# MLP entry of a hybrid decoder trunk: operand sums reordered, three kinds of sums moved to GpSimd, one buffer moved, lo*hi products last

## The chip, the cores and the metric

The kernel runs on one core of a Trainium2 chip. The metric is device microseconds of one launch, weights and input already in HBM. Three runs of the kernel before gave 2114.93, 2116.28 and 2116.18 us (median 2116.18).

## What is computed

Two decoder layers on 512 tokens of width 1024, all float32. Each layer: RMS norm, three parallel mixers, merge, output projection `w_out`, residual; then RMS norm and a gated MLP with a causal convolution:

```
x = x + merged @ w_out[l]
x = x + conv_ffn(rms_norm(x, ffn_norm_g[l]), w_up[l], conv_w[l], conv_b[l], w_down[l])

def conv_ffn(h, w_up, conv_w, conv_b, w_down):
    a, b = split(h @ w_up, 2, axis=-1)          # w_up is 1024 x 5632
    a = conv_b + sum(conv_w[j] * a shifted by 2 - j tokens for j in 0, 1, 2)
    return (silu(a) * b) @ w_down
```

The change touches the place where the second norm ends and `h @ w_up` begins, once per layer.

## The kernel before

Every float32 matrix product is made of three matmuls on split operands, x = hi + lo and w = hi + lo: hi·hi, hi·lo and lo·hi. ScalarE rounds to hi (`wsplit` line 163, `xsplit` line 506), VectorE subtracts to get lo (lines 164 and 507).

**The products of `w_up`.** For `h @ w_up` the kernel uses a seven-product scheme for 2x2 blocks in place of eight. x11 and x12 are tokens 0 to 255, with features 0 to 511 and 512 to 1023; x21 and x22 are tokens 256 to 511 with the same features. `fnorm_tile` (called for t = 0, 1, 2, 3, 128 tokens each) normalizes, transposes through TensorE into a `tp` bank of PSUM (two banks), and for t = 2 and 3 forms the sums s3 = x11 - x21, s1 = x22 - x21, s2 = -s1 - x11, s4 = -s2 - x12. All sums and all lo parts are VectorE's; the four operands "22", s1, s2, s3 lie in `hth`/`htl`, the others in tiles of their own (x11h, x12l, xs4h, xs4l). `ffn_quad` runs eleven times per layer (f = 0, 2, .. 20), each time over 256 columns of `w_up`: it loads four blocks of weights (w11, w12, w22, w21), forms four sums of them with `wsum` (VectorE, line 1111, into `tw` and in place), and calls `xprod` seven times with the operands "11", "s3", "s2", "12", "s1", "22", "s4". One `xprod` is 24 matmuls of 128x256 columns: for each half s and each k the three products in turn. x0 is the one PSUM bank with tag `o`; y0 and y1 are the two banks tagged `s`. `x0` of the next quad waits until `ua` (line 1139) has been copied out of it.

**Fillers.** For f = 0 `keep` issues twice eight bfloat16 matmuls that nobody reads (line 203), behind product "12" and behind the last transposes.

**Buffers.** `tw` is one of the six buffers tagged `raw`, in which the weight loads land too. The tag `gn` has one buffer: the norm's gain row.

**Order.** A framework takes the instructions in the order of the code and puts them, at build time, into one queue per engine, where it may move some ahead of others; each engine then works its queue strictly in order and waits on semaphores. `issue_after(i)` holds what is issued inside it behind instruction i. `later(2, rest)` puts the transposes and sums of a tile two steps later in the code.

Of the kernel before, what the change touches and what calls it, by code (L numbers as in the profile page):

```python
# [16 lines left out]
F32 = mybir.dt.float32  # L17
# [3 lines left out]
AF = mybir.ActivationFunctionType  # L21
ALU = mybir.AluOpType
AX = mybir.AxisListType.X
MUL, ADD, SUB, MAX, MIN = ALU.mult, ALU.add, ALU.subtract, ALU.max, ALU.min
# [24 lines left out]
class Stream:  # L49
# [3 lines left out]
    def __init__(self, gens, rate, depth=1):  # L53
        self.gens, self.rate, self.depth = gens, rate, depth
        self.credit, self.running = 0.0, []
# [29 lines left out]
class Net:  # L85
    def __init__(self, ctx, tc, io, out, depth, dbg=None):
        self.tc, self.nc, self.io, self.out, self.depth = tc, tc.nc, io, out, depth
        self.dbg = dbg or {}
        self.sb = ctx.enter_context(tc.tile_pool(name="sb", bufs=1))
        self.ps = ctx.enter_context(tc.tile_pool(name="ps", bufs=1, space=bass.MemoryType.PSUM))  # L90
        self.dr = ctx.enter_context(tc.tile_pool(name="dr", bufs=1, space=bass.MemoryType.DRAM))
        self.V, self.A, self.G, self.PE = tc.nc.vector, tc.nc.scalar, tc.nc.gpsimd, tc.nc.tensor
        self.specs = []
        self.after = []
        self.side, self.soon = [], []
        self.dq = tc.nc.sync
        self.n = 0

# [349 lines left out]
    def norm_rows(self, xt, t):  # L448

        V, A, G = self.V, self.A, self.G  # L450
        ss = self.small("nss", 2)
        for h in range(2):
            junk = self.slot("tmp", "junk")
            A.activation(junk, xt[t][h], AF.Square, accum_out=ss[:, h : h + 1])
        r = self.small("nr", 1)
        G.tensor_tensor(r, ss[:, 0:1], ss[:, 1:2], op=ADD)
        G.tensor_scalar(r, r, 1.0 / D, EPS, op0=MUL, op1=ADD)
        G.tensor_tensor(r, r, self.mhalf[:, 0:1], op=ALU.pow)
        hs = [self.slot("tmp", "hn") for _ in range(2)]
        for h in range(2):  # L460
            last = V.scalar_tensor_tensor(hs[h], xt[t][h], r, self.gn[:, h * 512 : h * 512 + 512], op0=MUL, op1=MUL)
        if self.after:
            self.after.append(last)
        return hs
# [32 lines left out]
        self.xop = ops  # L497
        self.x1 = self.slot("y4", "x11", (128, 4, 256)), self.slot("ct", "x12", (128, 4, 256))

    def xsplit(self, n, src, c):  # L500

        hi, lo = self.xop[n]
        w = 4 // len(hi)
        for i, (h, l) in enumerate(zip(hi, lo)):
            s = src[:, i * w : i * w + w]
            self.A.copy(h[:, :, c], s)
            self.V.tensor_tensor(l[:, :, c], s, h[:, :, c].bitcast(F32), op=SUB)

    def fnorm_tile(self, xt, t, wait=0):
        V, A = self.V, self.A  # L510
        hs = self.norm_rows(xt, t)
        x11, x12 = self.x1
        v4 = lambda a: a.rearrange("p (k q) -> p k q", k=4)

        def rest():
            c = slice((t % 2) * 128, (t % 2) * 128 + 128)
            tp = [v4(self.transpose4(hs[h])) for h in range(2)]
            if t < 2:
                for n, x, dst in zip(("11", "12"), tp, self.x1):
                    self.xsplit(n, x, c)  # L520
                    A.copy(dst[:, :, c], x)
                return
            x21, s3, s1, s2, s4 = (v4(self.slot("tmp", "xs")) for _ in range(5))
            A.copy(x21, tp[0])
            V.tensor_tensor(s3, x11[:, :, c], x21, op=SUB)
            self.xsplit("s3", s3, c)
            V.tensor_tensor(s1, tp[1], x21, op=SUB)
            V.scalar_tensor_tensor(s2, s1, -1.0, x11[:, :, c], op0=MUL, op1=SUB)
            self.xsplit("s2", s2, c)
            self.xsplit("s1", s1, c)  # L530
            self.xsplit("22", tp[1], c)
            V.scalar_tensor_tensor(s4, s2, -1.0, x12[:, :, c], op0=MUL, op1=SUB)
            self.xsplit("s4", s4, c)

        if wait:
            self.later(wait, rest)
        else:
            rest()
# [555 lines left out]
    def xprod(self, bank, w, n, start):  # L1094

        wh, wl = (x.rearrange("p (k f) -> p k f", k=4) for x in w)
        hi, lo = self.xop[n]
        per = 4 // len(hi)
        mm = self.PE.matmul
        for s in range(2):  # L1100
            o = bank[:, s * 256 : s * 256 + 256]
            fs = slice(s * 128, s * 128 + 128)
            for k in range(4):
                xh, xl = hi[k // per][:, k % per], lo[k // per][:, k % per]
                mm(o, lhsT=wh[:, k, fs], rhs=xh, start=start and s == k == 0, stop=False, skip_group_check=True)  # L1105
                mm(o, lhsT=wh[:, k, fs], rhs=xl, start=False, stop=False, skip_group_check=True)  # L1106
                last = mm(o, lhsT=wl[:, k, fs], rhs=xh, start=False, stop=k == 3, skip_group_check=True)  # L1107
        return last

    def wsum(self, out, a, b):  # L1110
        self.V.tensor_tensor(out, a, b, op=ADD)
        return out

    def ffn_quad(self, l, f, y0, y1, lo_out):


        V, A = self.V, self.A
        ca, cb = f * 128, DFF + f * 128
        w11 = self.load("s", "w_up", l, 0, ca)
        w12 = self.load("s", "w_up", l, 0, cb)  # L1120
        w22 = self.load("s", "w_up", l, 512, cb)
        tw = self.slot("raw", "tw", (128, 1024))
        w21 = self.load("s", "w_up", l, 512, ca)
        x0 = self.psum("o")
        self.xprod(x0, self.wsplit(w11), "11", True)
        A.copy(y0, x0)
        x1 = self.psum("tp")
        self.xprod(x1, self.wsplit(self.wsum(tw, w12, w22)), "s3", True)
        s7 = self.slot("tmp", "s7")
        A.copy(s7, x1)  # L1130
        self.xprod(y0, self.wsplit(self.wsum(tw, tw, w11)), "s2", False)
        A.copy(y1, y0)  # L1132
        last = self.xprod(x0, self.wsplit(w21), "12", False)
        if f == 0:
            self.keep(8, last)
            self.keep(8, self.last_tp)
        a = self.slot("ct", "ua", (128, 2, 512))
        half = lambda v: v.rearrange("p (s q) -> p s q", s=2)
        A.copy(a[:, :, :256], half(x0))
        self.xprod(y1, self.wsplit(self.wsum(w12, w12, w11)), "s1", False)  # L1140
        b2 = self.slot("tmp", "ub2")
        V.tensor_tensor(b2, y1, s7, op=ADD)
        self.xprod(y0, self.wsplit(self.wsum(tw, tw, w21)), "22", False)
        V.tensor_tensor(a[:, :, 256:], half(y0), half(s7), op=ADD)
        self.tick()
        self.xprod(y1, self.wsplit(w22), "s4", False)
        b1 = self.slot("tmp", "ub1")
        A.copy(b1, y1)
        y = self.slot("y4", "uy", (128, 2, 512))
        for s in range(2):  # L1150
            cw = lambda j: self.pk[:, l, PK_CW + 3 * (f + s) + j : PK_CW + 3 * (f + s) + j + 1]
            A.activation(y[:, s], a[:, s], AF.Identity, scale=cw(2), bias=self.pk[:, l, PK_CB + f + s : PK_CB + f + s + 1])
            V.scalar_tensor_tensor(y[:, s, 1:], a[:, s, :511], cw(1), y[:, s, 1:], op0=MUL, op1=ADD)
            V.scalar_tensor_tensor(y[:, s, 2:], a[:, s, :510], cw(0), y[:, s, 2:], op0=MUL, op1=ADD)
        A.activation(a, y, AF.Tanh, scale=0.5)
        V.scalar_tensor_tensor(y, a, 1.0, y, op0=ADD, op1=MUL)
        for h, b in enumerate((b1, b2)):
            yh = y[:, :, h * 256 : h * 256 + 256]
            V.tensor_tensor(yh, yh, half(b), op=MUL)
        gated = []  # L1160
        for s in range(2):
            hi, lo = self.slot("acc", "gh", dt=F32R), lo_out[:, s]
            A.activation(hi, y[:, s], AF.Copy, scale=-0.5)
            V.scalar_tensor_tensor(lo, y[:, s], -0.5, hi.bitcast(F32), op0=MUL, op1=SUB)
            gated.append((hi, lo))
        self.tick()
        return gated
# [242 lines left out]
```

## Time and profile before

| what | value |
|---|---|
| median of three runs | 2116.18 us |
| the profiled execution | 2114.53 us |
| its span, first to last instruction | 2112.8 us |
| TensorE (PE) busy | 2082.7 us, 99% |
| VectorE (DVE) busy | 1399.0 us, 66% |
| ScalarE (ACT) busy | 1002.1 us, 47% |
| GpSimd (POOL) busy | 156.4 us, 7% |

The profiled execution is 1.73 us longer than its span and 1.65 us below the median. A row of the timeline gives start, duration, engine, line, operation, out<-in, shape, and in brackets how long the engine had been idle before it and what released it. Durations overlap: an engine starts its next instruction before the last one's end, so that a 128x512 VectorE operation of 0.69 us costs 0.6 us of its queue and a 128x256 matmul of 0.28 us costs 0.12. The line "Lnnn" is of the kernel before; in the changed kernel the same code stands 1 to 12 lines further down.

### The profile page before, as it was taken

Reading aid. Unit: us, or ns where it says so; the run is one execution under the profiler, and the core shown is the slowest. Engines: PE = TensorE matmul, PEld = TensorE weight load, DVE = VectorE, ACT = ScalarE, POOL = GpSimd, SP = SyncE. Lnnn points to the kernel's source line nnn. Section 1 sums busy time; section 2 is a strip of 40 time slices with the busy share of each in tenths; the row PEclk is TensorE's granted clock in tenths of the full one; section 3 lists DMA queues with packets and bytes.
Section 4 is the critical chain, followed back from the end, with each engine's and each line's share of the span. In section 5 each row is a group of like instructions: output and inputs, shape, how many; then the busy total and the mean of one; then the engine's idle time right before and its main releaser. Section 6 shows DMA issues by size and latency. Waiting matters only on the chain.

```text
span 2112.8 us, 31791 instructions
## 1 busy us (share of the span) xinstructions
PE 2082.7 (99%) x12203; PEld 1821.6 (86%) x12203; DVE 1399.0 (66%) x2856; ACT 1002.1 (47%) x1981; POOL 156.4 (7%) x324
## 2 busy tenths in 40 slices
PE   9999999999999999999999999999999999999999
PEld 6877899988888799999878778999888888999997
DVE  7767565555645798888646675655565448987884
ACT  5355555553332555455443555454532326645552
POOL 1210112100000000000002111120000000000000
PEclk9999999999999999999999999999999999999999
DMA  6331222433332123323432311314334221333321
GB/s 211 99 94 39 70 78 63 121 123 102 138 100 74 66 95 120 110 92 108 154 111 72 101 41 61 96 46 143 110 100 146 94 70 56 105 110 111 110 91 70
DMA packets 97132, 206.09 MB, mean 98 GB/s; under 512 B 40530, under 2 KB 45394, under 8 KB 96980
## 3 DMA queue, kind: packets, MB, share of 16 engines
q1 hardware_dynamic: 96980, 204.06, 29.8%
q8 instruction: 96, 1.57, 0.3%
q14 instruction: 56, 0.46, 0.1%
HBM read 192.49 MB, written 11.53 MB: 97 GB/s over the span
## 4 chain that ended last, share of the span: by engine, by line
PE 87%; DVE 6%; ACT 4%; POOL 2%; issue 1%; DMA 1%; POOLq 0%; ACTq 0%; DVEq 0%
PE pacc L189 19%; PE pacc L188 19%; PE pacc L190 19%; PE ps L1105 4%; PE ps L1107 4%; PE ps L1106 4%; PE ptp L195 3%; PE po L1105 2%; PE po L1107 2%; PE po L1106 2%; PE ps L653 1%; PE po L750 1%; PE ptp L1106 1%; PE ptp L1105 1%; PE ptp L1107 1%
## 5 line engine op out<-in xcount | busy, mean ns | idle before, releaser
L164 DVE TENSOR_TENSOR wlo<-raw,whi 128x1024 fp32r<-128x1024 f32 x328 | 397.9, 1222 | 257.5 <-ACT whi L163 246.3
L163 ACT CAST whi<-raw 128x1024 fp32r<-128x1024 f32 x328 | 342.6, 1051 | 391.5 <-PE pacc L189 192.0
L188 PE MATMUL pacc<-whi,hth 128*128 128x512 f32 x768 | 319.1, 416 | 0.0
L189 PE MATMUL pacc<-wlo,hth 128*128 128x512 f32 x768 | 310.2, 404 | 3.2 <-DVE wlo L164 3.2
L190 PE MATMUL pacc<-whi,htl 128*128 128x512 f32 x768 | 310.9, 405 | 0.2 <-DVE htl L478 0.2
L189 PEld LDWEIGHTS pacc<-wlo,hth 128*128 128x128 f32 x768 | 192.6, 251 | 18.6 <-DVE wlo L164 4.1
L190 PEld LDWEIGHTS pacc<-whi,htl 128*128 128x128 f32 x768 | 191.7, 250 | 17.4 <-DVE htl L478 0.9
L188 PEld LDWEIGHTS pacc<-whi,hth 128*128 128x128 f32 x768 | 191.9, 250 | 15.7 <-ACT hth L477 0.4
L188 PE MATMUL pacc<-hth,whi 128*128 128x512 f32 x448 | 177.0, 395 | 0.0
L189 PE MATMUL pacc<-htl,whi 128*128 128x512 f32 x448 | 176.7, 394 | 0.0
L190 PE MATMUL pacc<-hth,wlo 128*128 128x512 f32 x448 | 174.6, 390 | 0.0
L1105 PE MATMUL ps<-hth,whi 128*128 128x256 f32 x528 | 148.3, 281 | 2.8 <-ACT ps L1132 2.8
L1107 PE MATMUL ps<-hth,wlo 128*128 128x256 f32 x528 | 147.6, 280 | 0.0
L1106 PE MATMUL ps<-htl,whi 128*128 128x256 f32 x528 | 147.6, 280 | 0.0
L189 PE MATMUL pacc<-wlo,gh 128*128 128x512 f32 x352 | 139.1, 395 | 0.0
L188 PE MATMUL pacc<-whi,gh 128*128 128x512 f32 x352 | 139.0, 395 | 0.0
L1105 PEld LDWEIGHTS ps<-hth,whi 128*128 128x128 f32 x528 | 99.2, 188 | 3.2 <-ACT ps L1132 3.2
L163 ACT CAST whi<-tw 128x1024 fp32r<-128x1024 f32 x66 | 69.3, 1049 | 67.3 <-PE po L1106 23.2
L188 PEld LDWEIGHTS pacc<-hth,whi 128*128 128x128 f32 x448 | 84.2, 188 | 19.1
L190 PEld LDWEIGHTS pacc<-hth,wlo 128*128 128x128 f32 x448 | 84.2, 188 | 18.5
L1107 PEld LDWEIGHTS ps<-hth,wlo 128*128 128x128 f32 x528 | 99.5, 188 | 0.0
L1106 PEld LDWEIGHTS ps<-htl,whi 128*128 128x128 f32 x528 | 98.9, 187 | 0.0
(373 smaller groups left out, 4675.0 us busy)
## 6 DMA issues: line engine op xcount, KB each, us to landing
raw<-wpk SPq DMA_DIRECT2D x328, 512.0 KB, 3.5
x<-x SPq DMA_DIRECT2D x16, 256.0 KB, 5.8
u_d<-uS SPq DMA_DIRECT2D x8, 256.0 KB, 2.4
u<-u_d SPq DMA_DIRECT2D x8, 256.0 KB, 3.4
y_d<-ys SPq DMA_DIRECT2D x8, 256.0 KB, 2.1
ym<-y_d SPq DMA_DIRECT2D x8, 256.0 KB, 4.0
um<-u_d SPq DMA_DIRECT2D x8, 256.0 KB, 3.4
oc_d<-glu SPq DMA_DIRECT2D x8, 256.0 KB, 2.0
```

Of the source, the lines that this page charges most:

```text
L163: self.A.copy(hi, raw)
L164: self.V.tensor_tensor(lo, raw, hi.bitcast(F32), op=SUB)
L188: self.PE.matmul(out, lhsT=ah, rhs=bh, start=i == 0, stop=False)
L189: self.PE.matmul(out, lhsT=ah, rhs=bl, start=False, stop=False)
L190: self.PE.matmul(out, lhsT=al, rhs=bh, start=False, stop=i == n - 1)
L195: self.last_tp = self.PE.transpose(tp[:, b * 128 : b * 128 + 128], src[:, b * 128 : b * 128 + 128], self.ident)
L653: PE.matmul(reg, lhsT=q[64 * j : 64 * j + 64, h * 128 : h * 128 + 128], rhs=k[kt][64 * j : 64 * j + 64, h * 128 : h * 128 + 128], start=kt ...
L750: PE.matmul(o[:, h * 128 : h * 128 + 128], lhsT=v[kb][:, h * 128 : h * 128 + 128], rhs=pT[:, c : c + 128], start=b == 0, stop=b == nb - 1)
L1105: mm(o, lhsT=wh[:, k, fs], rhs=xh, start=start and s == k == 0, stop=False, skip_group_check=True)
L1106: mm(o, lhsT=wh[:, k, fs], rhs=xl, start=False, stop=False, skip_group_check=True)
L1107: last = mm(o, lhsT=wl[:, k, fs], rhs=xh, start=False, stop=k == 3, skip_group_check=True)
```

## The change

It does five things. (1) `fnorm_tile` forms s3 of t = 2 and t = 3 first and puts all other sums of both into a list that is worked off after t = 3's; x22 is now copied from PSUM by ScalarE first. (2) x12 is kept negated, so that s4 = (-x12) - s2 is one plain subtraction, and s4 and its lo part are GpSimd's. (3) For f = 0 two of the four weight sums (w12 + w11 for product "s1", tw + w21 for product "22") are GpSimd's, held behind the last norm's reciprocal square root. (4) For f > 0 `tw` lies in the buffer `gn`. (5) `xprod` runs all eight hi·hi matmuls, then the eight hi·lo, then the eight lo·hi.

```diff
     def norm_rows(self, xt, t):
-        G.tensor_tensor(r, r, self.mhalf[:, 0:1], op=ALU.pow)
+        self.last_nr = G.tensor_tensor(r, r, self.mhalf[:, 0:1], op=ALU.pow)
...
-    def xsplit(self, n, src, c):
+    def xsplit(self, n, src, c, eng=None):
             self.A.copy(h[:, :, c], s)
-            self.V.tensor_tensor(l[:, :, c], s, h[:, :, c].bitcast(F32), op=SUB)
+            (eng or self.V).tensor_tensor(l[:, :, c], s, h[:, :, c].bitcast(F32), op=SUB)
...
-                    A.copy(dst[:, :, c], x)
+                    A.activation(dst[:, :, c], x, AF.Copy, scale=sign)
                 return
-            x21, s3, s1, s2, s4 = (v4(self.slot("tmp", "xs")) for _ in range(5))
+            x21, x22, s3 = (v4(self.slot("tmp", "xs")) for _ in range(3))
             A.copy(x21, tp[0])
             V.tensor_tensor(s3, x11[:, :, c], x21, op=SUB)
             self.xsplit("s3", s3, c)
-            V.tensor_tensor(s1, tp[1], x21, op=SUB)
-            V.scalar_tensor_tensor(s2, s1, -1.0, x11[:, :, c], op0=MUL, op1=SUB)
-            self.xsplit("s2", s2, c)
-            self.xsplit("s1", s1, c)
-            self.xsplit("22", tp[1], c)
-            V.scalar_tensor_tensor(s4, s2, -1.0, x12[:, :, c], op0=MUL, op1=SUB)
-            self.xsplit("s4", s4, c)
+            A.copy(x22, tp[1])
+
+            def sums():
+                s1, s2, s4 = (v4(self.slot("tmp", "xs")) for _ in range(3))
+                V.tensor_tensor(s1, x22, x21, op=SUB)
+                V.scalar_tensor_tensor(s2, s1, -1.0, x11[:, :, c], op0=MUL, op1=SUB)
+                self.xsplit("s2", s2, c)
+                self.xsplit("s1", s1, c)
+                self.xsplit("22", x22, c)
+                G.tensor_tensor(s4, x12[:, :, c], s2, op=SUB)
+                self.xsplit("s4", s4, c, G)
+
+            self.sums.append(sums)
+            if t == 3:
+                while self.sums:
+                    self.sums.pop(0)()
...
     def xprod(self, bank, w, n, start):
+        x = [(hi[k // per][:, k % per], lo[k // per][:, k % per]) for k in range(4)]
+        for part in range(3):
+            for s in range(2):
+                o = bank[:, s * 256 : s * 256 + 256]
+                fs = slice(s * 128, s * 128 + 128)
+                for k, (xh, xl) in enumerate(x):
+                    last = self.PE.matmul(o, lhsT=(wh, wh, wl)[part][:, k, fs], rhs=(xh, xl, xh)[part],
...
-    def wsum(self, out, a, b):
-        self.V.tensor_tensor(out, a, b, op=ADD)
+    def wsum(self, out, a, b, pool=False):
+        with ExitStack() as ctx:
+            if pool:
+                ctx.enter_context(self.tc.issue_after(self.last_nr.ins))
+            (self.G if pool else self.V).tensor_tensor(out, a, b, op=ADD)
...
-        tw = self.slot("raw", "tw", (128, 1024))
+        tw = self.slot("gn" if f else "raw", "tw", (128, 1024))
...
-        self.xprod(y1, self.wsplit(self.wsum(w12, w12, w11)), "s1", False)
+        self.xprod(y1, self.wsplit(self.wsum(w12, w12, w11, f == 0)), "s1", False)
...
-        self.xprod(y0, self.wsplit(self.wsum(tw, tw, w21)), "22", False)
+        self.xprod(y0, self.wsplit(self.wsum(tw, tw, w21, f == 0)), "22", False)
```

ScalarE's queue at the entry of layer 0, before (whi_7068 is hi of w12 + w11, whi_7019 of w21; xs_6857 and xs_6889 are x21 of t = 2 and 3; ps_6914 is y0; ua_7065 frees bank `o`):

```order
L163 CAST whi_7019<-raw_6925 128x1024
L163 CAST whi_7068<-raw_6920 128x1024
L524 COPY xs_6857<-ptp_6847 128x512
L1126 COPY ps_6914<-po_6927 128x512
L506 CAST hth_6423<-xs_6858 128x4x128
L506 CAST hth_6423<-xs_6859 128x4x128
L506 CAST hth_6423<-ptp_6852 128x4x128
```

The same place in the changed kernel (whi_7072 is hi of w12 + w11, whi_7103 of the sum for "22"):

```order
L164 CAST whi_7023<-raw_6929 128x1024
L164 CAST whi_7072<-raw_6924 128x1024
L525 COPY xs_6857<-ptp_6847 128x512
L1138 COPY ps_6918<-po_6931 128x512
L528 COPY xs_6858<-ptp_6852 128x512
L525 COPY xs_6875<-ptp_6865 128x512
L507 CAST hth_6423<-xs_6859 128x4x128
L507 CAST hth_6423<-xs_6858 128x4x128
L164 CAST whi_7103<-tw_6928 128x1024
L507 CAST hth_6423<-xs_6877 128x4x128
```

The cast of the sum w12 + w11 stands where it stood, ahead of the first copy out of the transposes' bank; before, its input (raw_6920) had come from VectorE, now (raw_6924) it comes from GpSimd. The cast of the sum for "22" has moved up from behind the last sum, to a place between the two casts of s3.

GpSimd's queue in the changed kernel, from the last norm on; before, the queue had nothing between nr_6839 and the next layer's memset (raw_6924 and tw_6928 are the weight sums, xs_6885 and xs_6901 are s4 of t = 2 and 3):

```order
L459 TENSOR_TENSOR nr_6839<-nr_6839,mhalf_83 128x1
L1123 TENSOR_TENSOR raw_6924<-raw_6924,raw_6922 128x1024
L1123 TENSOR_TENSOR tw_6928<-tw_6928,raw_6929 128x1024
L537 TENSOR_TENSOR xs_6885<-x_1354_6438,xs_6884 128x512
L508 TENSOR_TENSOR xs4l_6435<-xs_6885,xs4h_6433 128x2x128
L508 TENSOR_TENSOR xs4l_6436<-xs_6885,xs4h_6434 128x2x128
L537 TENSOR_TENSOR xs_6901<-x_1354_6438,xs_6900 128x512
L508 TENSOR_TENSOR xs4l_6435<-xs_6901,xs4h_6433 128x2x128
L508 TENSOR_TENSOR xs4l_6436<-xs_6901,xs4h_6434 128x2x128
```

Eight operations have come to GpSimd: two of 128x1024, two of 128x512 and four of 128x256.

TensorE's queue in the changed kernel, from the end of the fillers on (ptp_6961 is the bank of product "s3", ps_6918 is y0 and takes "s2", po_7188 is the next quad's bank `o`):

```order
L204 MATMUL pacc_7060<-identb_307 128x512
L1115 MATMUL ps_6918<-hth_6423,whi_6994 128x256 x8
L1115 MATMUL po_7188<-x11h_6425,whi_7189 128x256 x2
L1115 MATMUL ps_6918<-htl_6424,whi_6994 128x256 x8
L1115 MATMUL ps_6918<-hth_6423,wlo_6995 128x256 x8
```

Product "s3" now begins between the fillers, and the first two matmuls of the next quad stand inside product "s2"; before, they stood behind all seven products of the first quad.

## Rows read from the trace of the kernel before

**Rows 1.** The page's head and engines: busy us, share of the span, instructions.

```profile
span 2112.8 us, 31791 instructions
PE 2082.7 (99%) x12203; PEld 1821.6 (86%) x12203; DVE 1399.0 (66%) x2856; ACT 1002.1 (47%) x1981; POOL 156.4 (7%) x324
```

**Rows 2.** Windows at the two MLP entries: length, then busy us of each engine.

```profile
707.90:733.00 25.10, 21.10 (x155) 17.80 (x153) 22.56 (x33) 16.37 (x27) 1.35 (x3) 1.00 0.30 103
...
1757.30:1783.00 25.70, 21.55 (x159) 18.26 (x158) 23.16 (x33) 16.37 (x27) 1.35 (x3) 1.00 0.25 83
```

**Rows 3.** Timeline of TensorE at layer 0's entry: start, us, operation, [idle before <- releaser].

```profile
711.25 0.28 PE L1107 MATMUL po<-x11h,wlo 128*128 128x256 f32 x1
712.24 0.63 PE L195 MATMUL ptp<-identr,hn 128*128 128x128 f32 x4 [0.71 <-DVE hn L461]
...
713.94 0.39 PE L1107 MATMUL po<-x12h,wlo 128*128 128x256 f32 x1 [0.84 <-DVE wlo L164]
...
716.65 1.90 PE L203 MATMUL pacc<-identb 128*128 128x512 bf16 x8
718.78 0.63 PE L195 MATMUL ptp<-identr,hn 128*128 128x128 f32 x4 [0.23 <-DVE htl L507]
719.24 1.89 PE L203 MATMUL pacc<-identb 128*128 128x512 bf16 x8
...
722.36 0.39 PE L1106 MATMUL ptp<-htl,whi 128*128 128x256 f32 x1 [0.82 <-DVE htl L507]
...
725.18 0.28 PE L1105 MATMUL ps<-hth,whi 128*128 128x256 f32 x1
...
729.54 0.39 PE L1105 MATMUL ps<-hth,whi 128*128 128x256 f32 x1 [1.38 <-ACT ps L1132]
```

**Rows 4.** Timeline of ScalarE there.

```profile
709.61 1.98 ACT L163 CAST whi<-raw 128x1024 fp32r<-128x1024 f32 x2
711.50 0.57 ACT L524 COPY xs<-ptp 128x512 f32<-128x512 f32 x1
```

**Rows 5.** Timeline of VectorE there.

```profile
711.34 1.42 DVE L461 SCALAR_TENSOR_TENSOR hn<-x,nr,gn 128x512 f32<-128x512 f32 x2 [0.99 <-POOL nr L458]
712.67 1.22 DVE L164 TENSOR_TENSOR wlo<-raw,whi 128x1024 fp32r<-128x1024 f32 x1
713.80 0.69 DVE L525 TENSOR_TENSOR xs<-x,xs 128x512 f32<-128x512 f32 x1
```

**Rows 6.** GpSimd's groups by form: count, busy us, mean ns.

```profile
L965 POOL MEMSET toe<- 128x1024 f32 x8 | 7.6, 951 | 379.3 <-DVE uy L1156 321.1 <-PE ps L975 45.9 <-DMA raw<-wpk 12.3
L949 POOL MEMSET bblk<- 128x512 f32 x8 | 4.2, 524 | 0.1
```

**Rows 7.** Timeline of GpSimd and VectorE at the last two norms of layer 0.

```profile
702.46 0.19 POOL L456 TENSOR_TENSOR nr<-nss 128x1 f32<-128x1 f32 x1 [5.35 <-ACT junk L454]
...
709.12 1.23 DVE L164 TENSOR_TENSOR wlo<-tw,whi 128x1024 fp32r<-128x1024 f32 x1 [0.57 <-ACT whi L163]
...
709.78 0.61 POOL L456 TENSOR_TENSOR nr<-nss 128x1 f32<-128x1 f32 x1 [6.22 <-ACT junk L454]
...
710.75 0.55 POOL L458 TENSOR_TENSOR nr<-nr,mhalf 128x1 f32<-128x1 f32 x1
```

**Rows 8.** Timeline of GpSimd and VectorE around 97 us.

```profile
96.45 0.29 DVE L597 TENSOR_TENSOR rp<-qn,ropeA 128x128 f32<-128x128 f32 x1
96.63 1.80 POOL L587 TENSOR_SCALAR qr<-qs 128x8 f32<-128x8 f32 x1 [5.75 <-DVE qs L582]
...
98.07 0.29 DVE L894 TENSOR_TENSOR rot<-rt,rt 128x128 f32<-128x128 f32 x1
98.27 0.18 DVE L882 COPY curp<-ph 128x8 f32<-128x8 f32 x1
...
100.10 0.11 POOL L902 MEMSET d<- 128x4 f32 x1
```

**Rows 9.** Timelines of VectorE and TensorE further into the MLP, both layers.

```profile
805.74 1.23 DVE L1111 TENSOR_TENSOR tw<-raw,raw 128x1024 f32<-128x1024 f32 x1 [3.16 <-DMA raw<-wpk]
...
807.62 0.38 PE L1105 MATMUL ps<-xs4h,whi 128*128 128x256 f32 x1 [1.61 <-DVE ub L1142]
...
1855.60 0.39 PE L1105 MATMUL ps<-xs4h,whi 128*128 128x256 f32 x1 [0.34 <-DVE ub L1142]
```

More of the change, by code (lines that the diff above doesn't have):

```diff
@@ L95, in __init__ @@
         self.side, self.soon = [], []
+        self.sums = []
         self.dq = tc.nc.sync
@@ L506, in xsplit @@
             self.A.copy(h[:, :, c], s)
-            self.V.tensor_tensor(l[:, :, c], s, h[:, :, c].bitcast(F32), op=SUB)
+            (eng or self.V).tensor_tensor(l[:, :, c], s, h[:, :, c].bitcast(F32), op=SUB)
     def fnorm_tile(self, xt, t, wait=0):
-        V, A = self.V, self.A
+        V, A, G = self.V, self.A, self.G
         hs = self.norm_rows(xt, t)
@@ L518, in rest @@
             if t < 2:
-                for n, x, dst in zip(("11", "12"), tp, self.x1):
+                for n, x, dst, sign in zip(("11", "12"), tp, self.x1, (1.0, -1.0)):
                     self.xsplit(n, x, c)
-                    A.copy(dst[:, :, c], x)
+                    A.activation(dst[:, :, c], x, AF.Copy, scale=sign)
                 return
-            x21, s3, s1, s2, s4 = (v4(self.slot("tmp", "xs")) for _ in range(5))
+            x21, x22, s3 = (v4(self.slot("tmp", "xs")) for _ in range(3))
             A.copy(x21, tp[0])
@@ L1098, in xprod @@
         per = 4 // len(hi)
[L1099 to L1107, printed above, removed]
-        return last
-    def wsum(self, out, a, b):
-        self.V.tensor_tensor(out, a, b, op=ADD)
+        x = [(hi[k // per][:, k % per], lo[k // per][:, k % per]) for k in range(4)]
[5 more added lines that the diff above has]
+                    last = self.PE.matmul(o, lhsT=(wh, wh, wl)[part][:, k, fs], rhs=(xh, xl, xh)[part],
+                                          start=start and part == s == k == 0, stop=part == 2 and k == 3, skip_group_check=True)
+        return last
+    def wsum(self, out, a, b, pool=False):
[3 more added lines that the diff above has]
+            (self.G if pool else self.V).tensor_tensor(out, a, b, op=ADD)
         return out
```

## Prediction

> **What bounds the kernel now.** Read the page's engine line first [rows 1]: TensorE is busy 99% of the span, every other engine far less. A change that moves work between VectorE, ScalarE and GpSimd can only act where TensorE stands idle. The windows show where that is [rows 2]: in the 25.1 us of layer 0's MLP entry it is busy 21.10 us, so idle 4.0; at layer 1's entry 25.70 - 21.55 = 4.15. VectorE is busy 90% of these windows, against 66% over the whole span, and GpSimd 1.35 us. TensorE's timeline names the waits one by one [rows 3]: 0.71 us for the last norm, 0.84 for a lo part of weights, 0.23 and 0.82 for lo parts of s3 or its neighbours, 1.38 for the copy y1 <- y0. Together 3.98 us. The fillers (1.90 and 1.89 us) are also idle time in disguise, but the change keeps all sixteen. A second loss lies further on: a weight load comes 3.16 us late, and TensorE then waits 1.61 us in layer 0 and 0.34 in layer 1 [rows 9]. So the change works on 4.0 + 4.15 + 1.95 = 10.1 us, 0.48% of the time. That is the most it can win, and it wins that only if it adds no wait. A measurement of this kernel can tell about 0.2%, 4.2 us, from no change.
>
> **What costs nothing.** The same 24 matmuls per product run in another order, each still with its weight load, and TensorE takes one per 0.12 us there (23 steps from 722.36 to 725.18, [rows 3]), so (5) changes only when a lo part is needed: later, which removes the 0.84 us wait. The copy of x22 is a ScalarE copy of 0.57 us [rows 4] per tile that replaces nothing; ScalarE is busy 16.37 of 25.1 us [rows 2], but its queue order matters, below. The negated copy costs what the plain one did. `tw` in `gn` gives the loads all six `raw` buffers from the second quad on; I take the 1.95 us of [rows 9] as won. If another load is late instead, it is lost again.
>
> **What GpSimd pays.** It takes over two sums of 128x1024, two of 128x512 and four lo parts of 128x256 per layer. No row has such an operation on GpSimd. Nearest from below: a memset of 128x1024 takes 0.951 us and of 128x512 0.524 us [rows 6]; it only writes. From above: three such passes, two reads and a write without overlap, 2.85 us. The smallest two-operand operation takes 0.19 us [rows 7] where the smallest memset takes 0.11 [rows 8], a factor near two, so I take two passes: 1.9 us, 1.05 us, and 0.62 us for 128x256 (by the memsets' slope). VectorE does the two larger in 1.22 and 0.69 us [rows 5]. The Trainium skill, GPSIMD Engine Reference, section "Performance versus the Vector engine", has 4497 ns for a float32 addition of 2048 columns; half of it is 2.25 us, and by that the sum below would be 2.6 us larger. No run here shows it yet.
>
> **Do VectorE and GpSimd hold each other up?** This decides the sign. The first step of the norm on GpSimd takes 0.19 us at 702.46 but 0.61 at 709.78 [rows 7]. The second time VectorE's lo part, with two SBUF operands, ran from 709.12 to 710.35; GpSimd ended at 710.39. So GpSimd waits for such a VectorE operation to end. Around 97 us it fared worse [rows 8]: nine VectorE operations with two SBUF operands stood back to back from 96.45 on, and a GpSimd operation on eight columns took 1.80 us and ended only at 98.43, when they were through. At the entry all VectorE operations behind 711.3 have two SBUF operands, the "22" lo part too, now that x22 is read from SBUF. Whether VectorE waits for GpSimd in turn, no row shows: GpSimd has had no long read so far. I forecast that it does. The Trainium skill speaks against this change here: its page SBUF — State Buffer, section "Who interferes with whom", says that a VectorE instruction with two SBUF inputs and a GpSimd instruction that reads SBUF exclude each other, the second blocking until the first is done. The rows agree for one direction; by that rule the forecast below holds, without it the third or fourth rival.
>
> **The chain at layer 0, taking turns at 1.9 us.** *First wait.* The norm's last step ends at 711.30 [rows 7]; VectorE goes first with hn at 711.34, 0.66 us each in its queue [rows 5]. GpSimd sums w12 + w11 from 712.0 to 713.9. ScalarE's queue has the cast of this sum directly ahead of the copy out of the transposes' bank, as the order shows; before, that input had long been there. Cast 0.95 us, copy 0.57 [rows 4]: 715.5. TensorE, done at 711.53, stands 4.0 us in place of 0.71 [rows 3]. *Second.* "12" with both transposes takes 3.57 + 0.46 us (712.24 to 716.65 less 0.84; 718.78 to 719.24) [rows 3] and one filler 0.24: 719.8. VectorE meanwhile: hn to 714.55, GpSimd's second sum to 716.45, then in VectorE's queue lo of w21 1.13, s3 0.6, lo of the sum 1.13, lo of s3 0.6, s3 of t = 3 0.6: 720.55, ScalarE's cast 0.6: 721.2. Wait 1.4. *Third.* Product s3 (2.8) and fifteen fillers (3.5) end at 727.55. VectorE goes through six operations (4.1 us), lo of s1 0.6, s4 on GpSimd 1.05, s1 0.6, GpSimd's lo part 0.62, VectorE's 0.6, GpSimd's 0.62, s2 of t = 3 0.6: 729.4, cast 0.6: 730.0. Wait 2.45. *Fourth.* Eight matmuls to 730.95; then stand two of the next quad, which need bank `o`, which needs `ua`, which stands in ScalarE's queue behind the casts of the last s4: GpSimd to 731.05, casts and copy 1.25: 732.3. Wait 1.35. *Fifth.* The lo part of s2 of t = 3 comes behind a weights' lo part (1.13) and a GpSimd turn (0.62): 733.5, TensorE is there at 732.55. Wait 0.95.
>
> Sum 10.15 us against 3.98, +6.2; layer 1, with 4.15 before, +6.0. Less 1.95 for the load: **+10.2 us**. The profiled execution took 2114.53 us, 1.65 below the median; with it 2124.7, and I give **2125 us**. Per layer 3.76 sums' worth of GpSimd lie on this chain (two sums, 0.55 twice for s4, 0.33 twice for lo parts), so the bounds of the price give: at 0.95 us, 7.1 us less, 2117.6; at 2.85 us, 7.1 more, 2132.
>
> **The rivals.**
> 1. *GpSimd starves.* As around 97 us, it gets in only when VectorE stops. First sum 713.85 to 715.75, copy out at 717.3, wait 5.75. VectorE then has some twenty operations (15.2 us) before it needs anything from GpSimd; only then s4 and its lo parts come (3.35 us), casts and `ua` 1.2, to 737.2, with TensorE there at about 729: wait 8.2. (14 - 4) x 2 - 2 = +18: 2132.5. For it: [rows 8]. Against it: at 709.78 GpSimd got in at the first operation's end, though nothing stood behind that one.
> 2. *It collides nowhere, at 1.9 us.* First sum 711.4 to 713.3, copy out 714.85: wait 3.3. The last s4 ends near 725.5, `ua` near 726.7, a wait of 0.3 to 1.2. (4.1 - 4.05) x 2 - 1.95 = -1.9: 2112.6, no change that can be told. Against it: both rows of waiting.
> 3. *Faster: GpSimd as quick as its memset, and no collision.* The sum ends at 712.35, copy out 713.9, wait 2.4, and all five old waits go. (2.4 - 4.05) x 2 - 1.95 = -5.2: 2109.3. It decides from a price of about 1.2 us downward, and only if VectorE isn't held. For it: VectorE, the fullest engine here, loses two sums of 1.13 and two of 0.6 us and four lo parts per entry.
>
> **How the numbers follow.** Taking turns 0.45, starving 0.20, no collision 0.17, faster 0.18. Within the first case a price under 1.1 us stays inside 4.2 us; I give that 0.05. So slower 0.40 + 0.20 = 0.60, same 0.17 + 0.05 = 0.22, faster 0.18. The likeliest case alone runs from 2117.6 to 2132. The range, 2111 to 2134, adds the second rival and the first; it leaves out most of the third and starving at a higher price.
>
> **What would show it.** TensorE's first wait at the entry: 4 us or more, with ScalarE's cast released by GpSimd ahead of it; 2.4 or less speaks for the third rival. GpSimd's 128x1024 rows: near 1.9 us or longer where VectorE runs. VectorE idle, or its lo parts stretched, while GpSimd sums. A second new wait of TensorE at the next quad's bank `o`. The late load and its 1.61 us gone. The prediction is wrong if GpSimd's sums and VectorE's operations overlap in full at their usual lengths.

## The result and the profile after

| | before | after |
|---|---|---|
| median of six runs each | 2115.22 us | 2129.27 us |
| the profiled execution, its span | 2114.53, 2112.8 | 2129.02, 2127.2 |
| start to the first matmul of the MLP in layer 0 | 707.99 | 707.86 |
| from there to the same place in layer 1 | 1049.20 | 1055.93 |
| from there to the end | 355.61 | 363.41 |

The changed kernel takes 1.0068 times as long (95% interval 1.0057 to 1.0078), 14.05 us more. The forecast was 2125, the range 2111 to 2134. The three lower rows divide the profiled span at the timeline's first matmul of the MLP (`ps<-identr`): 6.7 us were lost in layer 0, 7.8 in layer 1, nothing ahead of them.

The page's head of the changed kernel, against [rows 1]:

```profile
span 2127.2 us, 31836 instructions
PE 2089.6 (98%) x12203; PEld 1829.1 (86%) x12203; DVE 1406.2 (66%) x2840; ACT 1007.0 (47%) x1985; POOL 186.9 (9%) x340
```

TensorE is busy 6.9 us longer than before with the same 12203 matmuls: not all of the loss is waiting. VectorE has 16 instructions fewer and is busy 7.2 us longer. TensorE's timeline at layer 0's entry, against [rows 3]:

```profile
710.29 1.10 PE L1115 MATMUL po<-x11h,wlo 128*128 128x256 f32 x8
715.09 1.00 PE L196 MATMUL ptp<-identr,hn 128*128 128x128 f32 x4 [3.70 <-ACT xs L525]
715.74 1.42 PE L1115 MATMUL po<-x12h,whi 128*128 128x256 f32 x5
...
721.57 1.21 PE L1115 MATMUL ptp<-hth,whi 128*128 128x256 f32 x8 [0.73 <-ACT hth L507]
...
729.20 1.21 PE L1115 MATMUL ps<-hth,whi 128*128 128x256 f32 x8 [1.18 <-ACT hth L507]
733.71 0.80 PE L1115 MATMUL po<-x11h,whi 128*128 128x256 f32 x2 [3.30 <-ACT ua L1151]
734.30 1.91 PE L1115 MATMUL ps<-htl,whi 128*128 128x256 f32 x8
736.01 1.91 PE L1115 MATMUL ps<-hth,wlo 128*128 128x256 f32 x8
...
740.02 1.10 PE L1115 MATMUL ps<-htl,whi 128*128 128x256 f32 x8
...
747.56 1.10 PE L1115 MATMUL po<-x11l,whi 128*128 128x256 f32 x8
```

and at layer 1's:

```profile
1771.08 1.11 PE L196 MATMUL ptp<-identr,hn 128*128 128x128 f32 x4 [3.76 <-ACT xs L525]
...
1785.18 1.21 PE L1115 MATMUL ps<-hth,whi 128*128 128x256 f32 x8 [1.18 <-ACT hth L507]
1789.69 0.80 PE L1115 MATMUL po<-x11h,whi 128*128 128x256 f32 x2 [3.30 <-ACT ua L1151]
```

In layer 0 four waits, 8.91 us in place of 3.98; in layer 1 three, 8.24 in place of 4.15. Behind layer 0's last wait eight matmuls take 1.91 us (734.30 and 736.01), where eight of the same kind take 1.10 at 740.02: 0.21 us a step in place of 0.12. Behind the first, five take 1.42 us (715.74), where the same five take 0.85 in the run no_gpsimd below. The windows name the reason (the number ahead of the last two is the granted clock, the mean of the stretch):

```profile
716.00:720.00 4.00, 4.00 (x26) 3.96 (x26) 4.00 (x5) 2.06 (x5) 0.24 (x1) 0.66 0.30 95
...
728.00:732.00 4.00, 1.23 (x9) 1.00 (x8) 4.00 (x4) 1.63 (x4) 4.00 (x3) 1.00 0.00 0
732.00:736.00 4.00, 2.29 (x10) 2.29 (x11) 3.96 (x4) 1.19 (x3) 3.49 (x3) 0.54 0.38 131
736.00:740.00 4.00, 4.00 (x23) 4.00 (x23) 1.94 (x2) 1.53 (x2) 0.38 (x1) 0.60 0.00 0
740.00:744.00 4.00, 4.00 (x36) 4.00 (x35) 3.49 (x4) 1.06 (x2) 0.00 (x0) 1.00 0.23 57
```

Behind TensorE's 3.70 us of idling the granted clock is 0.66, behind the 3.30 us it is 0.54 and 0.60, mostly the lower level (1.2 GHz), and from 740 on it is 1.00 (2.4 GHz). The price of both together is read at the ninth matmul of the second quad. Before, that one was:

```profile
739.08 0.28 PE L1107 MATMUL po<-x11h,wlo 128*128 128x256 f32 x1
```

From the first matmul of the MLP to there layer 0 takes 39.70 us (707.86 to 747.56; before 707.99 to 739.08, 31.09). Of these 8.61 us more, 4.93 are waits. The other 3.68 are matmuls at the lower level: without its waits the stretch takes 30.8 us, before 27.1, and in no_gpsimd, at a granted clock of 1.00, 27.0. Layer 1 the same way: 8.2, of which 4.1 and 4.1. What the table shows is less by about what the late load gives back further on (1.61 and 0.34 us before).

What the long waits hang on is in the rows of GpSimd:

```profile
711.14 2.34 POOL L1123 TENSOR_TENSOR raw<-raw,raw 128x1024 f32<-128x1024 f32 x1
713.44 2.80 POOL L1123 TENSOR_TENSOR tw<-tw,raw 128x1024 f32<-128x1024 f32 x1
725.14 2.20 POOL L537 TENSOR_TENSOR xs<-x,xs 128x512 f32<-128x512 f32 x1 [8.91 <-PE ptp L1115]
```

of ScalarE:

```profile
713.51 1.04 ACT L164 CAST whi<-raw 128x1024 fp32r<-128x1024 f32 x1 [2.99 <-POOL raw L1123]
714.46 0.58 ACT L525 COPY xs<-ptp 128x512 f32<-128x512 f32 x1
...
732.46 0.71 ACT L507 CAST xs4h<-xs 128x256 fp32r<-128x256 f32 x2 [2.83 <-POOL xs L537]
733.08 0.58 ACT L1151 COPY ua<-po 128x512 f32<-128x512 f32 x1
```

and of VectorE, against [rows 5]:

```profile
711.21 5.59 DVE L462 SCALAR_TENSOR_TENSOR hn<-x,nr,gn 128x512 f32<-128x512 f32 x2 [1.00 <-POOL nr L459]
716.71 1.21 DVE L165 TENSOR_TENSOR wlo<-raw,whi 128x1024 fp32r<-128x1024 f32 x1
...
725.54 0.68 DVE L532 TENSOR_TENSOR xs<-xs,xs 128x512 f32<-128x512 f32 x1
726.14 1.75 DVE L508 TENSOR_TENSOR htl<-xs,hth 128x512 fp32r<-128x512 f32 x1
...
729.55 1.76 DVE L165 TENSOR_TENSOR wlo<-raw,whi 128x1024 fp32r<-128x1024 f32 x1
```

So the first long wait comes about like this: GpSimd's first sum ends at 713.48, ScalarE has waited 2.99 us to cast it, and only behind this cast comes the copy out of the transposes' bank, which lets TensorE go on at 715.09. ScalarE's order is not all of it. The first `hn`, which the same transposes need, ends only at 714.04 (by their tile, the two `hn` take 2.82 and 2.84 us each), so with the copy in time TensorE would still have stood 2.65 of the 3.70 us. A cast put behind the copy was not tried. The last wait: ScalarE has waited 2.83 us for GpSimd's second s4 (until 732.43), `ua` comes behind its casts, and TensorE goes on at 733.71.

The two `hn`, 1.42 us before, take 5.59 while GpSimd makes its two sums: 4.17 us more, 2.1 for each sum. A lo part of 0.68 us takes 1.75 beside s4, one of 1.21 takes 1.76 beside a lo part of s4: the s4 sum holds VectorE for 1.07 us, a 128x256 lo part for 0.55.

### The profile page after: what moved, and what is told of

Its sections match the earlier page's. It is cut to its first block, busy times and chain, and to the rows that moved or that the text cites. A ratio compares the mean times of both kernels' runs of the same rounds, so it can differ in the third digit from the quotient of the medians.

```text
span 2127.2 us, 31836 instructions
## 1 busy us (share of the span) xinstructions
PE 2089.6 (98%) x12203; PEld 1829.1 (86%) x12203; DVE 1406.2 (66%) x2840; ACT 1007.0 (47%) x1985; POOL 186.9 (9%) x340
## 4 chain that ended last, share of the span: by engine, by line
PE 88%; DVE 5%; ACT 4%; POOL 2%; issue 1%; ACTq 0%; DVEq 0%; POOLq 0%
PE pacc L189 19%; PE pacc L190 19%; PE pacc L191 19%; PE ps L1115 12%; PE po L1115 5%; PE ptp L1115 3%; PE ptp L196 2%; PE ps L663 1%; PE po L760 1%; PE ps L736 1%; DVE wlo L165 1%; PE ps L988 1%; ACT qn L604 1%; POOL qr L598 1%; DVE hn L462 1%
## 5 line engine op out<-in xcount | busy, mean ns | idle before, releaser
L190 PEld LDWEIGHTS pacc<-htl,whi 128*128 128x128 f32 x448 | 84.3, 188 | 16.5
L165 DVE TENSOR_TENSOR wlo<-tw,whi 128x1024 fp32r<-128x1024 f32 x66 | 80.5, 1220 | 17.5 <-ACT whi L164 17.5
L1208 DVE TENSOR_TENSOR x<-x,pacc 128x512 f32<-128x512 f32 x96 | 65.1, 682 | 21.7 <-PE pacc L191 21.7
L189 PEld LDWEIGHTS pacc<-whi,gh 128*128 128x128 f32 x352 | 66.1, 188 | 15.4 <-DVE x L1208 0.6
L190 PEld LDWEIGHTS pacc<-wlo,gh 128*128 128x128 f32 x352 | 65.9, 187 | 15.1
L598 POOL TENSOR_TENSOR qr<-qr,mhalf 128x4 f32<-128x4 f32 (+1 forms) x64 | 76.3, 1192 | 5.3
```

The source lines that it names most:

```text
L165: self.V.tensor_tensor(lo, raw, hi.bitcast(F32), op=SUB)
L189: self.PE.matmul(out, lhsT=ah, rhs=bh, start=i == 0, stop=False)
L190: self.PE.matmul(out, lhsT=ah, rhs=bl, start=False, stop=False)
L598: G.tensor_tensor(r, r, self.mhalf[:, :heads], op=ALU.pow)
L1208: self.V.tensor_tensor(xt[t][s], xt[t][s], acc, op=ADD)
```

## The experiments

Medians; the kernel before measured 2114.7 to 2115.3 beside these runs.

### Which of GpSimd's two jobs costs what

**s4_vector** gives s4 back to VectorE:

```diff
-                G.tensor_tensor(s4, x12[:, :, c], s2, op=SUB)
-                self.xsplit("s4", s4, c, G)
+                V.tensor_tensor(s4, x12[:, :, c], s2, op=SUB)
+                self.xsplit("s4", s4, c)
```

> The changed kernel, but s4 and its lo part are VectorE's again; the two weight sums stay on GpSimd. Theory (each of GpSimd's two jobs makes one long wait, and TensorE runs at the 1.2 GHz level after each): the first wait stays at 3.7 us and the slow microseconds behind it, the wait of 3.3 us for bank o goes, and the slow matmuls behind it. Waits about 6.4 us per layer in place of 8.9, some 2 us per layer less at the low clock: 2129.3 - 2 x 4.5 = about 2120 us. Rival A (the wait for bank o is only inherited: VectorE is late because the weight sums held it): it stays, 2128 to 2130 us.

Measured 2119.01 us. The first wait stays 3.70 us, with a granted clock of 0.58 behind it (716 to 720); the wait for bank `o` is gone, and no slow matmul is left behind the place where it was.

**wsum_vector** gives the weight sums back:

```diff
-        self.xprod(y1, self.wsplit(self.wsum(w12, w12, w11, f == 0)), "s1", False)
+        self.xprod(y1, self.wsplit(self.wsum(w12, w12, w11)), "s1", False)
...
-        self.xprod(y0, self.wsplit(self.wsum(tw, tw, w21, f == 0)), "22", False)
+        self.xprod(y0, self.wsplit(self.wsum(tw, tw, w21)), "22", False)
```

> The changed kernel, but all weight sums are VectorE's again; s4 and its lo part stay on GpSimd. Theory: the first wait falls to 0.7 to 0.9 us as before, with no slow stretch behind it. If s4 on GpSimd makes its wait by itself, 3.3 us and its slow stretch stay: 2129.3 - 2 x (2.9 + 1.9) = about 2120 us. Rival A (that wait is inherited): all long waits go, the time is 2112 to 2116 us.

Measured 2119.31 us. The first wait is 0.70 us; rival A falls. The wait that s4 makes has moved: ScalarE's casts of s2 and s1 stand behind those of s4, and TensorE waits 2.45 us for s2's hi and 1.54 for its lo, with slow matmuls after. GpSimd and VectorE there:

```profile
720.30 3.40 POOL L537 TENSOR_TENSOR xs<-x,xs 128x512 f32<-128x512 f32 x1 [8.07 <-DVE xs L533]
```

```profile
720.09 0.69 DVE L508 TENSOR_TENSOR htl<-xs,hth 128x512 fp32r<-128x512 f32 x1
720.69 0.68 DVE L532 TENSOR_TENSOR xs<-xs,xs 128x512 f32<-128x512 f32 x1
721.29 0.69 DVE L508 TENSOR_TENSOR htl<-xs,hth 128x512 fp32r<-128x512 f32 x1
721.89 0.68 DVE L533 SCALAR_TENSOR_TENSOR xs<-xs,x 128x512 f32<-128x512 f32 x1
724.99 3.47 DVE L508 TENSOR_TENSOR htl<-xs,hth 128x512 fp32r<-128x512 f32 x3 [2.41 <-ACT hth L507]
```

A subtraction of 1.1 us takes 3.40: four VectorE operations went through first, and after the fourth VectorE had nothing ready until 724.99. GpSimd does not get every second turn.

**no_gpsimd** makes both edits.

> The changed kernel with neither job on GpSimd: what is left is the new order of the sums, x22 copied by ScalarE, tw in the buffer gn, and the lo*hi matmuls last. Theory (all of the loss is GpSimd's): no wait over 1.5 us at the entries, granted clock 1.00, some 3.3 us of waits per layer against 4.0 before, and the late load gone (1.95 us): 2115.2 - 1.3 - 1.95 = about 2112 us. Rival B (the new order itself costs): 2118 us or more.

Measured 2109.26 us, ratio to before 0.9973 (0.9962 to 0.9984): faster than both kernels, granted clock 1.00, waits 0.71, 0.59, 0.18 and 1.15 in layer 0. The two jobs cost 10.3 and 10.0 us one by one, 20.0 together: they add up. The rest of the change gains 6.0 us. Rival B falls.

### Is it holding, or only waiting for slow results?

**unread_sums** adds GpSimd work to no_gpsimd that nobody uses:

```diff
+            d = self.slot("acc", "dmy")
+            with self.tc.issue_after(self.last_nr.ins):
+                for h in (0, 512, 0, 512):
+                    self.G.tensor_tensor(d, self.gn[:, h : h + 512], self.gn[:, h : h + 512], op=ADD)
```

> no_gpsimd plus, per layer, four additions of 128x512 on GpSimd (the gain row to itself, into a buffer that nobody reads), issued behind the last norm's reciprocal square root, where the changed kernel has its two weight sums. The queues of TensorE, VectorE and ScalarE hold the same instructions in the same order as in no_gpsimd, and no engine waits for a result of these four, so whatever changes is contention. Theory (a GpSimd operation on SBUF and a VectorE operation with two SBUF operands run one after the other): each addition takes 1.1 us, and VectorE stretches by about that at hn and the operations behind it; its queue, full up to s2, comes 4.4 us later, and TensorE with it: 2109.3 + 2 x 4.4 = about 2118 us, up to 2121 us with slow matmuls behind the longer wait. Rival D (the loss is only that somebody waits for GpSimd's slow results): VectorE's hn keeps its 0.7 us, 2109 to 2110 us.

Measured 2116.24 us, 7.0 more than no_gpsimd. VectorE and GpSimd:

```profile
711.29 2.96 DVE L462 SCALAR_TENSOR_TENSOR hn<-x,nr,gn 128x512 f32<-128x512 f32 x2 [1.00 <-POOL nr L459]
714.17 2.06 DVE L165 TENSOR_TENSOR wlo<-raw,whi 128x1024 fp32r<-128x1024 f32 x1
716.16 1.52 DVE L526 TENSOR_TENSOR xs<-x,xs 128x512 f32<-128x512 f32 x1
```

```profile
711.22 5.91 POOL L1140 TENSOR_TENSOR dmy<-gn 128x512 f32<-128x512 f32 x4
```

`hn`, the lo part and s3 take 1.55, 0.84 and 0.83 us more than in no_gpsimd, and TensorE starts s2 3.2 us later in layer 0 and 4.2 in layer 1. Rival D falls.

**unread_memsets** puts writes in their place:

```diff
-                for h in (0, 512, 0, 512):
-                    self.G.tensor_tensor(d, self.gn[:, h : h + 512], self.gn[:, h : h + 512], op=ADD)
+                for _ in range(8):
+                    self.G.memset(d, 0.0)
```

> As unread_sums, but GpSimd writes zeros (eight memsets of 128x512 per layer, 0.52 us each by rows 6, 4.2 us in all) in place of adding: it occupies GpSimd for about as long, and reads nothing. The queues of TensorE, VectorE and ScalarE are again those of no_gpsimd. Theory (it is GpSimd's reading of SBUF that excludes VectorE): hn keeps 0.7 us apiece, the time is that of no_gpsimd, 2109 to 2110 us. Rival E (any GpSimd operation of that length holds VectorE): as unread_sums, 2116 us.

Measured 2109.84 us, that of no_gpsimd:

```profile
711.10 4.61 POOL L1140 MEMSET dmy<- 128x512 f32 x8
```

```profile
711.18 1.41 DVE L462 SCALAR_TENSOR_TENSOR hn<-x,nr,gn 128x512 f32<-128x512 f32 x2 [1.00 <-POOL nr L459]
```

GpSimd is busy for 4.61 us, and `hn` takes 1.41. So GpSimd's writing alone does not hold VectorE; what the additions have besides is their reads (and the arithmetic, which no run takes apart from them). The Trainium skill, SBUF — State Buffer, section "Who interferes with whom", says just this: a VectorE instruction with two SBUF inputs contends with a GpSimd instruction that reads SBUF, not with one that only writes. Both runs agree with it.

### The clock

**fill_idle** puts fillers into the two long waits (and holds the last tile's transposes behind the first of them):

```diff
+        if f == 0:
+            with self.tc.issue_after(self.keep(14, last).ins):
+                self.flush()
...
+        if f == 0:
+            self.keep(12, self.hihi)
```

> The changed kernel with 14 more bfloat16 fillers held between product 11 and the last tile's transposes, and 12 more behind product s2, for f = 0; GpSimd's work is untouched. TensorE is kept busy (each filler 0.24 us) where it stood idle for 3.7 and 3.3 us. Theory (the matmuls of 0.21 us a step are the price of the idle stretches before them): granted clock 1.00 at both entries, every x12h and hth matmul at 0.12 us a step, and since the fillers lie in time that was idle the kernel gets 4 to 8 us faster in spite of 6.1 us more of them per layer: 2121 to 2125 us. Rival C (the slow matmuls come from something else, such as the weights being read while GpSimd works): they stay slow, the time is 2129 us or more.

Measured 2139.57 us: the total was missed. The build moved all other fillers behind product s2 and the operand sums further back, so that TensorE waited 3.39 us elsewhere. The first stretch still answers the question; beside the fillers only the place of four transposes differs there:

```profile
711.37 3.19 PE L204 MATMUL pacc<-identb 128*128 128x512 bf16 x14
715.23 0.65 PE L196 MATMUL ptp<-identr,hn 128*128 128x128 f32 x4 [0.67 <-ACT xs L526]
...
717.45 1.19 PE L1116 MATMUL po<-x12h,whi 128*128 128x256 f32 x8
...
723.43 2.08 PE L1116 MATMUL ptp<-hth,whi 128*128 128x256 f32 x8 [3.39 <-ACT hth L508]
```

```profile
716.00:720.00 4.00, 2.94 (x24) 2.81 (x24) 4.00 (x5) 2.54 (x5) 0.36 (x1) 1.00 0.32 84
```

The transposes come as late as in the changed kernel, GpSimd's sums run as there, the granted clock is 1.00, and the matmuls take 0.12 to 0.13 us a step. Behind the wait of 3.39 us they are slow, though GpSimd does nothing from 716.36 to 726.13. Rival C falls for these places.

**no_fillers** takes the sixteen fillers out of no_gpsimd:

```diff
-            self.keep(8, last)
-            self.keep(8, self.last_tp)
+            pass
```

> no_gpsimd without the sixteen fillers. VectorE sets when s3 and s2 are ready, so TensorE stands idle for the same time, now in one stretch of 0.59 + 0.94 = 1.5 us ahead of s3 and one of 0.18 + 2.83 = 3.0 us ahead of s2. Theory (idle stretches of about 3 us and more cost twice, by the wait and by slow matmuls after it): the granted clock falls behind the second stretch, product s2 goes at 0.21 us a step, up to 24 x 0.09 = 2.2 us per layer: 2111 to 2114 us. Rival (the fillers buy nothing): granted clock 1.00, 2109.3 us.

Measured 2111.63 us, 2.4 more than with them (1.9 by the two ratios to the kernel before). TensorE's timeline:

```profile
718.29 1.21 PE L1115 MATMUL ptp<-hth,whi 128*128 128x256 f32 x8 [1.39 <-ACT hth L507]
...
724.39 2.07 PE L1115 MATMUL ps<-hth,whi 128*128 128x256 f32 x8 [2.79 <-ACT hth L507]
726.26 1.91 PE L1115 MATMUL ps<-htl,whi 128*128 128x256 f32 x8
```

```profile
724.00:728.00 4.00, 3.61 (x17) 3.61 (x18) 4.00 (x8) 2.70 (x6) 0.00 (x0) 0.50 0.00 0
```

No GpSimd sum runs here, and behind the longer idle stretch the granted clock is 0.50 and the matmuls are slow all the same: the slow step is TensorE's clock, not GpSimd's. Not every wait has this price: behind 2.39 us in unread_sums the granted clock stayed at 1.00, and the first eight matmuls took 1.21 us as in no_gpsimd.

### The parts that gain

**only_gn_buffer** is the kernel before with `tw` in `gn`.

```diff
-        tw = self.slot("raw", "tw", (128, 1024))
+        tw = self.slot("gn" if f else "raw", "tw", (128, 1024))
```

> The kernel before with one part of the change: tw lies in the buffer gn from the second quad on. Expected by the prediction's term: the load that came 3.16 us late comes in time, and the waits of 1.61 and 0.34 us go: 2115.3 - 1.95 = 2113.3 us. Otherwise another load is late, and nothing changes: 2115.3 us.

Measured 2112.63 us, -2.4 (expected -1.95): both waits of [rows 9] are gone.

**only_lo_last** is the kernel before with the new `xprod` alone.

> The kernel before with one part of the change: xprod runs hi*hi, hi*lo and lo*hi one after the other. The waits for a lo part at the second and third matmul (0.84 and 0.82 us in layer 0, 0.83 twice in layer 1) go, as these are needed 8 to 16 matmuls (0.9 to 1.9 us) later: 2115.3 - 3.3 = 2112 us if nothing else waits. If VectorE's full queue sets the pace the wait moves to the copy y1 <- y0 behind it, and the time stays at 2115 us.

Measured 2110.17 us, -4.9, more than expected. The waits for lo parts inside a product are gone, layer 0's entry waits 0.71, 1.32 and 0.73 us, and the late load costs 1.2 in place of 1.61. These make some 3 us; where the rest comes from was not tried.

**gn_and_lo_last** is both.

> The kernel before with two parts of the change together: tw in gn (alone -2.4 us) and the lo*hi matmuls last (alone -4.9 us); the order of the operand sums is the old one. If the two are independent: 2115.1 - 7.3 = 2107.8 us, and the new order of the sums, which no_gpsimd (2109.3 us) has besides, is worth nothing or costs 1 to 2 us. If the new order is what no_gpsimd lives on, this stays at 2110 us or more.

Measured 2109.47 us, 1.7 us above the sum of the two gains (2.1, by the kernel before beside it at 2114.72). 0.45 us of that is what only_lo_last had already taken off the late load; its runs scatter from 2108.7 to 2110.6, and the rest stays open. It equals no_gpsimd (2109.26): the new order of the sums is worth nothing that can be measured.

### A better order?

**vector_order** reorders VectorE's queue and drops the fillers; its core:

```diff
+                s = [p[0]() for p in self.sums]
+                with self.tc.issue_after(self.last_s2.ins):
+                    for j in (1, 2):
+                        for p, a in zip(self.sums, s):
+                            p[j](*a)
```

(`p[0]` forms s1 and s2 of a tile, `p[1]` splits s2, `p[2]` s1 and 22; s4 follows the sum for 22. The edit also holds the lo part of w12 + w11, the sum for 22 and the second quad's first weight sum behind the last s2.)

> no_gpsimd with VectorE's queue put in the order in which TensorE needs the results: behind the last hn and the lo part of w21 first all of s3, s1 and s2 of both tiles, then the lo parts of s2, s1 and 22, the lo part of w12 + w11, the sum for 22, and s4 last; the sixteen fillers are taken out. Nothing is on GpSimd. Theory (VectorE's queue up to s2 sets when TensorE gets on): the lo part of w12 + w11 (1.14 us), of 22 and s1 (0.6 each), s4 (0.6) and its lo parts (0.66) no longer stand ahead of s2, which comes 3.6 us earlier; TensorE then waits 0.7 + 0.5 + 0.2 + 1.15 us per layer in place of 2.6 us of waits and 3.8 us of fillers: 2109.3 - 2 x 3.9 = about 2101.5 us, 2100 to 2104 us, granted clock 1.00. Rival (ScalarE's queue of casts and copies sets it, or what is put back is late for s1, 22 and s4): 2107 us or more.

Measured 2118.97 us. The first quad came out as expected (TensorE reached s2 at 719.76, in no_gpsimd at 723.66), the second did not: its first weight sum, which this edit holds back too, had fallen behind the first quad's convolution in VectorE's queue (to 735.85).

```profile
738.45 1.38 PE L1129 MATMUL ptp<-hth,whi 128*128 128x256 f32 x8 [2.56 <-ACT whi L164]
```

A second wait of 2.7 us follows it, and slow matmuls behind both. What was won at the entry was lost one quad later. Whether a better place for that sum keeps the gain was not tried.

**late_lo** moves one instruction of gn_and_lo_last:

```diff
-        self.xprod(y1, self.wsplit(self.wsum(w12, w12, w11)), "s1", False)
+        w12 = self.wsum(w12, w12, w11)
+        with ExitStack() as ctx:
+            if f == 0:
+                ctx.enter_context(self.tc.issue_after(self.last_s2.ins))
+            w12 = self.wsplit(w12)
+        self.xprod(y1, w12, "s1", False)
```

> gn_and_lo_last with one instruction held back: the lo part of w12 + w11 (1.14 us of VectorE's queue, wanted only by product s1) is issued behind the last s2 instead of ahead of the lo part of s3. In VectorE's queue another operation of the same length, the sum for product 22, comes up into the place that it leaves; the two matmuls' worth of the next quad's product 11 come to stand behind s2, where TensorE waited 0.73 us for the copy y1 <- y0. If that wait goes in both layers: 2109.5 - 1.5 = 2108 us, 2107 to 2109 us; if VectorE's queue is as full as before: 2109.5 us.

Measured 2108.42 us, ratio to before 0.9967 (0.9955 to 0.9980): 6.6 us faster than before and the lowest median of all, though no_gpsimd and gn_and_lo_last, 0.8 and 1.0 us above it, lie within its interval. The wait for y1 <- y0 is gone in both layers, one of 0.3 us has come at s3.

## Why the prediction was right, and where it was off

**Sign and cause: right, and shown.** It rested on VectorE and GpSimd excluding each other both ways, for which it had rows for one way only. unread_sums shows the other, and unread_memsets shows that writing alone does not do it. The second and third rival fall with that (the passage on the Trainium skill calls them the third and fourth).

**GpSimd's price.** Taken at 1.9, 1.05 and 0.62 us; measured 2.34, 1.07 and 0.55. The interpolation was good for the smaller and short for the 128x1024 sum, by 0.4 of its row and by 0.2 of what it cost VectorE (2.1). The estimate from the Trainium skill's figure (GPSIMD Engine Reference, "Performance versus the Vector engine"), half of 4497 ns, was 2.25 us: there the page was nearer.

**The first wait: right in size (4.0; 3.70), wrong in order.** The step "VectorE goes first with hn at 711.34" failed: GpSimd's sum started at 711.14, ahead of it; the norm's last step runs on GpSimd itself, directly ahead of the sum. That gained 0.86 us, the price lost 0.44. By its length alone the wait tells little, as 3.70 lies between the forecast's 4.0 and the second rival's 3.3; what tells them apart is `hn`, held for 4.17 us. And the forecast had ScalarE's cast as the only link; the held `hn` alone would have made 2.65 us.

**The second to fifth wait: 6.15 us forecast, 5.21 measured, otherwise spread.** The step that failed is "taking turns" after every VectorE operation. At 725.14 GpSimd waited for two operations, in wsum_vector for four. So s2 of t = 3 came earlier than forecast (third wait 1.18, not 2.45; no fifth), and s4 of t = 3 and `ua` behind it later (fourth 3.30, not 1.35). The starving rival, by which GpSimd gets in only when VectorE stops, describes wsum_vector's 3.40 us; here GpSimd got in after two operations with a third one ready, and the first weight sum ahead of both `hn`.

**The missing term.** The forecast counted waits and took every matmul at 0.12 us. Behind the waits of 3.70 and 3.30 us, and their likes in layer 1, the granted clock went to the lower level: 3.7 us in layer 0, 4.1 in layer 1, 7.8 in all; fill_idle and no_fillers tie that to the idling. Waits by themselves rose by 4.9 and 4.1, where +6.2 and +6.0 were forecast. 10.2 - 3.2 + 7.8 is 14.8, against 14.4 between the two profiled executions. The forecast of 2125 is 2114.53, the profiled execution, plus 10.2; that execution became 2129.02, 14.5 more. It came this near by luck: a term too large and a term left out partly cancelled.

**The late load: right.** Both of its waits are gone; alone the edit gains 2.4 us, forecast 1.95.

**"What costs nothing": too small.** The new order inside a product was credited with one wait of 0.84 us, though the 0.82 us in the same rows is a wait for a lo part inside a product, too, and went as well; alone it gains 4.9 us. The forecast let GpSimd's waits swallow all of the old ones, which was so, but missed that the other parts are by themselves the better change: without GpSimd they gain 6.0 us.

## What to carry to other kernels

Before moving work from a full VectorE to an idle GpSimd, look whether both read SBUF at once: if VectorE's operations have two SBUF operands, the moved work stays in VectorE's time, here at nearly twice its price (1.07 us in place of 0.6 for 128x512). That VectorE operations with an operand in PSUM would have gone through was not tried. Price a new wait of TensorE with the matmuls behind it, too: here the four long waits of both layers came to 14.1 us, and the matmuls at the lower clock behind them added 7.8. And when a change is a bundle, run the parts: here two cheap ones gain, and moving work to GpSimd loses over three times as much.

## What was not expected of the hardware

GpSimd's turn is not fair: its 128x512 operation of 1.1 us took 2.20 us behind two VectorE operations and 3.40 behind four, the second time only when VectorE had nothing ready, yet the unread sums got in after each single one (5.91 us for four, with four VectorE operations stretched by some 0.8 us each). What decides between these was not tried.

The first 700 us differ by up to 1.3 us from one execution to the next with nothing changed there (first matmul of the MLP between 707.83 and 709.09); in only_gn_buffer, wsum_vector and gn_and_lo_last the granted clock was 0.66 from 10 to 20 us, where it is 1.00 in before. Effects of that size need the medians, not one profile.
